# A ReGLU MLP on one core: the first set's x loaded in whole rows and turned on TensorE, later x loaded and turned in quarters of a set

## The chip, the cores and the metric

The kernel runs on one core of a Trainium2 chip. The metric is device time in microseconds (us). Every time quoted without another word is the median of a kernel's runs in one series.

A ratio is the mean time of one kernel's fast runs over the mean of the other's fast runs of the same rounds, so it is not quite the ratio of the medians. It comes with a 95% interval.

PE is TensorE's matmuls, PEld its weight loads, DVE is VectorE, ACT is ScalarE, POOL is GpSimd, and SP is the engine that issues most transfers. A profile is one execution. The profiled run of the kernel before took 369.32 us, longer than each of its timed runs. The span that a profile shows is about 2 us shorter than the device time.

## The reference

```python
batch, seq, dim, hidden = 16, 256, 512, 2048        # x: 16*256 = 4096 tokens, all float32

def reference(x, w1, w2):
    h = x @ w1                                      # 4096x512 @ 512x4096
    gate, value = np.split(h, 2, axis=-1)
    h = np.maximum(gate, 0) * value
    return (h @ w2).astype(np.float32)              # 4096x2048 @ 2048x512
```

## The kernel before

The 4096 tokens are worked in four *sets* of 1024. Each set has two stages.

- **Product blocks.** There are sixteen, one for each 128 hidden columns. A *plain* block does 16 matmuls of 128x512. A *Winograd* block treats (two halves of the tokens) x (gate, value) as a 2x2 product and needs seven products of two matmuls each, 14 in all. For that it needs sums of x (S1 to S4) and of w1 (T1 to T4). The result, after max and multiply, is `g`.
- **The second matmul**, `g` by w2, in tiles named `O`. It is 128 matmuls per set: ten are mixed into the set's own last blocks, 114 form one long run, and four are left to be mixed into the next set's blocks. I call that long run and its surroundings a **set boundary**: from its first matmul to the first product of the next set. During it the next set's x must be brought in, turned and summed.

The matmuls of this kernel take x *turned*: tokens along the row, dimensions on the partitions. Before the change DVE did that with a block transpose, after a load in pieces of 128 numbers (512 bytes).

```python
stage = tile_pool(bufs=1)      # one staging tile: 8 KB per partition, half a set of x
tmp   = tile_pool(bufs=5)      # five temporaries of 4 KB: turned x AND output tiles o
psx = (bufs=3, PSUM); psy = (bufs=3, PSUM); psw = (bufs=2, PSUM)    # X and O share psx

def x_ops(s, eng):                                   # next set's x, at the boundary; eng = POOL
    o = x_tiles()
    t1 = load_x(s, 0, x_tile())                      # first half of the set
    yield o
    a11 = turn(x_tmp(), t1, 0)                       # DVE, 128x1024
    nc.scalar.copy(out=o["A11"], in_=a11)            # ACT
    a12 = turn(x_tmp(), t1, 1)
    nc.scalar.copy(out=o["A12"], in_=a12)
    t2 = load_x(s, 1, x_tile())                      # second half: the SAME staging tile
    yield o
    a21 = turn(x_tmp(), t2, 0)
    a22 = turn(x_tmp(), t2, 1)
    eng.tensor_tensor(o["S1"], a21, a22, op=ADD)     # POOL, reads the turned temporaries
    eng.tensor_tensor(o["S3"], a11, a21, op=SUB)
    nc.scalar.copy(out=o["A22"], in_=a22)            # ACT
    yield o
    eng.tensor_tensor(o["S2"], f(o["S1"]), a11, op=SUB)
    eng.tensor_tensor(o["S4"], a12, f(o["S2"]), op=SUB)
    yield o

# ... mm2_stream: 16 matmuls into one O tile, then
            o = tmp.tile([P, DO], F32, name="o", tag="tmp")
            nc.scalar.copy(out=o, in_=ps)            # ACT
            nc.sync.dma_start(out=out_v[s, b], in_=o)

# ... end of a set
        gen = x_ops(s + 1, nc.gpsimd)
        for xo in gen:
            advance(stream, 10)                      # ten O matmuls, then the next part of x_ops
        advance(stream, NB * NJ - TAIL - 50)
```

The first set starts with four plain blocks, which do not need the sums. (`# ...` marks cuts; the pool lines are shortened.)

## Time and profile before

| | before |
|---|---|
| time | 367.63 us (367.53 to 368.49, 3 runs) |
| TensorE busy | 92% of the span |
| three set boundaries, each needing 24.4 us for its matmuls | 32.38, 31.64, 32.85 us |
| first product of the first set | 13.0 us |
| long O run of the first set begins | 77.1 us |

The first lines are from the profile's page of the kernel before: busy time of the engines, then PE's busy share and granted clock in 40 equal slices, one digit each in tenths.

```profile
PE 339.1 (92%) x1428; PEld 208.9 (57%) x1454; DVE 199.7 (54%) x270; ACT 151.1 (41%) x261; POOL 78.2 (21%) x58
...
PE   7969999996799999999499999999589999999995
PEclk9999999999699999999899999999969999999998
```

After the first set (its start, and stalls at 6 tenths in the third slice), TensorE is nearly always busy except at three spots (6, 4 and 5 tenths), and at or just after each of them its clock falls too. Those spots are the boundaries. The next lines, from the same page, give the chain of work that ended last, and the group of O matmuls: busy us, mean ns of one, then the idle time just before them and what ended it.

```profile
PE 72%; DMA 11%; DVE 7%; POOL 4%; ACT 2%; SPq 2%; issue 1%; DVEq 0%; ACTq 0%
...
L218 PE MATMUL O<-w_sb,g 128*128 128x512 bf16 x500 | 120.5, 396 | 16.6 <-ACT o L230 16.0
```

The waits view of PE gives who waited, for what, total us, number of waits, longest.

```profile
PE O L218 <- ACT o L230: 16.0, 3, 5.4
...
PE X L206 <- ACT x_A_182 L302: 1.3, 1, 1.3
PE X L206 <- ACT x_S_185 L299: 1.1, 1, 1.1
```

"PE waits for ACT's copy of an O tile" is true and misleading: the copy takes 0.58 us and the wait 5.3. One has to look at what stood *in front of* that copy. The timeline of the first boundary shows it (columns: start us, us, engine, line, operation, count; in brackets the idle time of that engine before, and what ended it):

```profile
77.10 11.83 PE L218 MATMUL O<-w_sb,g 128*128 128x512 bf16 x53
...
81.96 1.91 SPq L83 DMA_DIRECT2D xs<-in_x_dram  x4
...
88.67 3.85 DVE L87 STREAM_TRANSPOSE xt<-xs 128x1024 f32<-128x1024 f32 x2 [6.75 <-DMA xs<-in_x_dram]
92.56 1.04 ACT L116 CAST x_A_707<-xt 128x1024 fp32r<-128x1024 f32 x1 [9.55 <-DVE xt L87]
...
93.51 0.58 ACT L230 COPY o<-O 128x512 f32<-128x512 f32 x1
...
94.14 15.70 PE L218 MATMUL O<-w_sb,g 128*128 128x512 bf16 x59 [5.21 <-ACT o L230]
```

Read it from below. PE resumes at 94.14, when the O copy at 93.51 is done. That copy was queued on ACT behind the copy of A22 at 92.56, which ended 9.55 us of idle time. The A22 copy waited for DVE's turn. DVE had idled 6.75 us for the second half of x. That load was issued only at 81.96, because the one staging tile was held by the first half until it was turned. Meanwhile three PSUM tiles of O filled up and PE stopped. In this trace ACT did not let the O copy pass: its tile had long been finished, and it started 0.95 us after the start of the A22 copy and not before it.

### The profile page before, as it was taken

The numbers are of one execution on the slowest core, as the hardware profiler recorded it, in microseconds if no ns is written. First come the engines' busy times: TensorE is split into PE (matmuls) and PEld (weight loads), VectorE is DVE, ScalarE is ACT, GpSimd is POOL, SyncE is SP. The second block draws the span as 40 slices with busy tenths as digits, with TensorE's granted clock in tenths as the row PEclk, the third lists the DMA queues.
The fourth block names the chain that finished last, engine by engine and source line by source line (L and its number), as shares of the span: only waits on it lengthen the run. The fifth ranks groups of instructions, "written<-read, shape, count | busy, mean of one in ns | idle before, by whom it ended". The sixth has DMA issues, their size and how long they took to land.

```text
span 367.5 us, 3904 instructions
## 1 busy us (share of the span) xinstructions
PE 339.1 (92%) x1428; PEld 208.9 (57%) x1454; DVE 199.7 (54%) x270; ACT 151.1 (41%) x261; POOL 78.2 (21%) x58
## 2 busy tenths in 40 slices
PE   7969999996799999999499999999589999999995
PEld 4547566642246777764146777774234777775442
DVE  0588676873005887773402887776400687886000
ACT  2558767520316545522214455542032555552111
POOL 1259989800910000000450000000090000000000
PEclk9999999999699999999899999999969999999998
DMA  9973687905225000006132400001422000000212
GB/s 190 273 221 116 202 206 114 166 29 116 86 86 133 11 0 0 3 0 139 35 114 68 105 2 0 0 2 53 89 87 86 31 0 1 2 0 2 86 62 80
DMA packets 33139, 27.51 MB, mean 75 GB/s; under 512 B 1248, under 2 KB 29152, under 8 KB 33120
## 3 DMA queue, kind: packets, MB, share of 16 engines
q1 hardware_dynamic: 29824, 24.52, 24.6%
q0 software_dynamic: 2112, 2.10, 3.6%
q10 hardware_dynamic: 1184, 0.66, 0.7%
q8 instruction: 11, 0.18, 0.2%
q14 instruction: 8, 0.07, 0.1%
HBM read 20.97 MB, written 8.39 MB: 80 GB/s over the span
## 4 chain that ended last, share of the span: by engine, by line
PE 72%; DMA 11%; DVE 7%; POOL 4%; ACT 2%; SPq 2%; issue 1%; DVEq 0%; ACTq 0%
PE O L218 23%; PE Y L153 22%; PE W L153 14%; PE X L153 13%; DVE xt L87 6%; DMA w_sb<-in_w_dram 6%; DMA xs<-in_x_dram 4%; SPq L83 2%; POOL w_T_84 L135 1%; POOL w_T_85 L136 1%; POOL w_T_87 L138 1%; POOL w_T_86 L137 1%; ACT o L230 0%; ACT w_B_82 L270 0%; ACT x_A_1925 L116 0%
## 5 line engine op out<-in xcount | busy, mean ns | idle before, releaser
L218 PE MATMUL O<-w_sb,g 128*128 128x512 bf16 x500 | 120.5, 396 | 16.6 <-ACT o L230 16.0
L218 PEld LDWEIGHTS <-g 128*128 128x128 bf16 x512 | 50.3, 101 | 83.0 <-issue 31.3
L180 DVE TENSOR_TENSOR cc<-W,pu 128x512 f32<-128x512 f32 x60 | 41.5, 691 | 97.8 <-ACT pu L174 96.0
L160 ACT COPY Y<-X 128x512 f32<-128x512 f32 x60 | 34.3, 572 | 49.7 <-PE X L153 43.3
L174 ACT COPY pu<-Y 128x512 f32<-128x512 f32 x60 | 35.2, 587 | 37.7 <-PE Y L153 37.6
L230 ACT COPY o<-O 128x512 f32<-128x512 f32 x31 | 18.1, 585 | 69.7 <-PE O L218 59.9
L87 DVE STREAM_TRANSPOSE xt<-xs 128x1024 f32<-128x1024 f32 x14 | 27.5, 2000 | 28.5 <-DMA xs<-in_x_dram 28.5
L181 DVE SCALAR_TENSOR_TENSOR g<-X,cc 128x512 bf16<-128x512 f32 x60 | 41.5, 691 | 2.3
L190 DVE SCALAR_TENSOR_TENSOR g<-Y,cc 128x512 bf16<-128x512 f32 x60 | 40.8, 680 | 3.3 <-PE Y L153 3.3
L186 DVE TENSOR_TENSOR cc<-Y,pu 128x512 f32<-128x512 f32 x60 | 40.9, 681 | 0.8 <-PE Y L153 0.3
L167 ACT COPY pu<-W 128x512 f32<-128x512 f32 x60 | 35.2, 587 | 0.0
L114 POOL TENSOR_TENSOR x_S_1317<-xt 128x1024 fp32r<-128x1024 f32 x1 | 2.3, 2341 | 77.8 <-DVE xt L87 77.8
L114 POOL TENSOR_TENSOR x_S_1926<-xt 128x1024 fp32r<-128x1024 f32 x1 | 2.3, 2343 | 76.9 <-DVE xt L87 76.9
L153 PEld LDWEIGHTS <-w_B_82 128*128 128x128 bf16 x120 | 7.2, 98 | 16.6 <-issue 15.9
L227 DVE COPY o<-O 128x256 f32<-128x256 f32 x1 | 0.4, 425 | 25.2 <-ACT o L225 25.2
L153 PE MATMUL Y<-x_S_1318,w_T_85 128*128 128x512 f32 x32 | 13.0, 487 | 0.0
L153 PE MATMUL Y<-x_S_709,w_T_85 128*128 128x512 f32 x32 | 13.0, 487 | 0.0
L153 PE MATMUL Y<-x_S_1927,w_T_85 128*128 128x512 f32 x32 | 13.0, 486 | 0.0
L135 POOL TENSOR_TENSOR w_T_84<-w_sb 128x512 fp32r<-128x512 f32 x6 | 8.7, 1456 | 8.6 <-DMA w_sb<-in_w_dram 8.6
L153 PE MATMUL X<-x_A_1314,w_B_81 128*128 128x512 f32 x32 | 10.3, 404 | 0.0
L153 PE MATMUL X<-x_A_1923,w_B_81 128*128 128x512 f32 x32 | 10.3, 404 | 0.0
L153 PE MATMUL X<-x_A_705,w_B_81 128*128 128x512 f32 x32 | 10.3, 403 | 0.0
(126 smaller groups left out, 509.8 us busy)
## 6 DMA issues: line engine op xcount, KB each, us to landing
out_dram<-o SPq DMA_DIRECT2D x31, 256.0 KB, 2.0
xs<-in_x_dram SPq DMA_DIRECT2D x28, 256.0 KB, 4.9
w_sb<-in_w_dram SPq DMA_DIRECT2D x7, 1024.0 KB, 6.6
w_sb<-in_w_dram POOLq DMA_DIRECT2D x4, 512.0 KB, 9.2
g<-in_x_dram SPq DMA_DIRECT2D x4, 256.0 KB, 8.0
w_sb<-in_w_dram ACTq DMA_DIRECT2D x1, 512.0 KB, 6.5
w_sb<-in_w_dram SPq DMA_DIRECT2D x1, 512.0 KB, 8.6
out_dram<-o ACTq DMA_DIRECT2D x1, 128.0 KB, 1.8
```

Of the source, the lines that this page charges most:

```text
L87: nc.vector.transpose(a.rearrange("p b (tb r) -> p b tb r", r=32), t.rearrange("p tb (c k b) -> p k b tb c", k=2, b=2)[:, k])
L135: nc.gpsimd.tensor_tensor(op["T1"], b12, b11, op=SUB)
L153: nc.tensor.matmul(ps, wop[wn][:, b, self.jb * P:(self.jb + 1) * P], self.xo[xn][:, b, :], start=fresh and b == 0, stop=b == 1, skip_group ...
L160: nc.scalar.copy(out=self.Y, in_=self.X)
L167: nc.scalar.copy(out=self.p5, in_=self.W)
L174: nc.scalar.copy(out=self.u2, in_=self.Y)
L180: nc.vector.tensor_tensor(self.c12, self.W, self.u2, op=ADD)
L181: nc.vector.scalar_tensor_tensor(out=self.g[:, self.jb, :TH], in0=self.X, scalar=0.0, in1=self.c12, op0=MAX, op1=MULT)
L186: nc.vector.tensor_tensor(self.c22, self.Y, self.p5, op=ADD)
L190: nc.vector.scalar_tensor_tensor(out=self.g[:, self.jb, TH:], in0=self.Y, scalar=0.0, in1=self.c22, op0=MAX, op1=MULT)
L218: nc.tensor.matmul(ps, g[:, hc, b * P:(b + 1) * P], w2_sb[:, hc, :], start=hc == 0, stop=hc == NJ - 1)
L230: nc.scalar.copy(out=o, in_=ps)
```

## The change

Its intent: fill the staging earlier and in smaller pieces, so that the boundary has no late load; turn the first set's x on TensorE, which is idle or only warming up then, from loads of whole rows (2 KB); use two plain blocks instead of four. The warm-up matmuls at the start are also changed (30 instead of 38; not shown). The diff, cut to its core:

```diff
-NPLAIN = 4
+NPLAIN = 2
-    stage = ... bufs=1        # 8 KB tile
-    tmp = ... bufs=5
+    stage = ... bufs=3        # 4 KB tiles, a quarter of a set each
+    tmp = ... bufs=4
...
+    HOME = {(0, 0): "A11", (0, 1): "S4", (1, 0): "S3", (1, 1): "A22"}
+    def x_sums(o, engines):          # sums read the copied tiles, not the turned temporaries
+        a11, a22, s1, s2, s3, s4 = (f(o[n]) for n in ("A11", "A22", "S1", "S2", "S3", "S4"))
+        for eng, n, i0, i1, op in zip(engines, ("S1", "S2", "S4", "S3"), (s3, s1, s4, a11), (a22, a11, s2, s3),
+                                      (ADD, SUB, SUB, SUB)):
+            yield eng.tensor_tensor(o[n], i0, i1, op=op)
...
+    def turn_x(o, t, i):             # one quarter: two turns of 128x512, two copies
+        ts = slice(i % 2 * 256, i % 2 * 256 + 256)
+        for k in range(2):
+            a = tmp.tile([P, 2, 256], F32, name="xt", tag="tmp")
+            nc.vector.transpose(a..., t...[:, k])
+            nc.scalar.copy(out=o[HOME[i // 2, k]][:, :, ts], in_=a)
+        if i == 1:
+            nc.scalar.copy(out=o["A12"], in_=f(o["S4"]))
...
+    def turn_first(o, h):            # first set, half h: 16 transposes on TensorE
+        for b in range(4):
+            pool, nm = (psx, "X") if b % 2 else (psw, "W")
+            ps = pool.tile([P, TH], F32, name=nm, tag=nm)
+            for e in range(4):
+                nc.tensor.transpose(ps[:, e * P:(e + 1) * P], xn[h][:, b]...[:, e], ident)
+            for k, copy in ((0, nc.vector.tensor_copy), (1, nc.scalar.copy)):
+                copy(out=o[HOME[h, k]][:, :, b * P:(b + 1) * P], in_=ps[...])
...                                   # preamble: half 0 turned, plain 0 and 1, half 1 turned,
+    sums = x_sums(xo, (nc.vector,) * 4)      # then four sums on DVE among plain 0 and 1
...
+                if n == "P1" and jb in (9, 11, 13) and s + 1 < NS:
+                    xs.append(load_x(s + 1, len(xs)))       # three quarters during the last blocks
...
-            gen = x_ops(s + 1, nc.gpsimd)
-            for xo in gen:
-                advance(stream, 10)
-            advance(stream, NB * NJ - TAIL - 50)
+            xo = x_tiles()
+            turn_x(xo, xs[0], 0)
+            advance(stream, 6)
+            turn_x(xo, xs[1], 1)
+            xs.append(load_x(s + 1, 3))                     # fourth quarter: a staging tile is free now
+            advance(stream, 12)
+            turn_x(xo, xs[2], 2)
+            advance(stream, 18)
+            turn_x(xo, xs[3], 3)
+            for _ in x_sums(xo, (nc.gpsimd,) * 4):
+                pass
+            advance(stream, NB * NJ - TAIL - 46)
```

More of the change, by code (lines that the diff above doesn't have):

```diff
@@ L6 @@
 from concourse._compat import with_exitstack
+from concourse.masks import make_identity
 dt = mybir.dt
@@ L16 @@
 PERIOD = 7
-NWARM = 38
-NPLAIN = 4
+NWARM = 30
+NPLAIN = 2
 SLOT = {"P1": 0, "P5": 1, "P2": 3, "P6": 4, "P3": 5, "P7": 9, "P4": 13}
@@ L44 @@
     gpool = ctx.enter_context(tc.tile_pool(name="gpool", bufs=1))
-    stage = ctx.enter_context(tc.tile_pool(name="stage", bufs=1))
-    tmp = ctx.enter_context(tc.tile_pool(name="tmp", bufs=5))
+    stage = ctx.enter_context(tc.tile_pool(name="stage", bufs=3))
+    tmp = ctx.enter_context(tc.tile_pool(name="tmp", bufs=4))
     psx = ctx.enter_context(tc.tile_pool(name="psx", bufs=3, space=bass.MemoryType.PSUM))
@@ L65 @@
     warm_b = warm.rearrange("p a t -> p (a t)").bitcast(BF16)
-    warm_r = warm.rearrange("p a t -> p (a t)").bitcast(F32R)
-    nc.vector.memset(warm, 0.0)
+    nc.vector.memset(warm[:, 0], 0.0)
+    ident = wpool.tile([P, P], F32, name="ident")
     for i in range(NWARM):
-        pool, nm = (((psy, "Y"),) * 3 + ((psx, "X"),) * 3 + ((psw, "W"),) * 2)[i % 8]
+        pool, nm = (psy, "Y") if i < 16 else (psx, "X")
         t = pool.tile([P, TH], F32, name=nm, tag=nm)
-        m = P // 2 if 18 <= i < 26 else P
-        if i < 10 or i >= 26 and i % 2:
-            nc.tensor.matmul(t, warm_b[:, :P], warm_b[:, :TH], start=True, stop=True)
-        else:
-            nc.tensor.matmul(t[:m], warm_r[:, :m], warm_r[:, TH:], start=True, stop=True)
+        n = TH if i < 16 else TH // 2
+        nc.tensor.matmul(t[:, :n], warm_b[:, :P], warm_b[:, :n], start=True, stop=True)
     def f(ap):
         return ap.bitcast(F32)
-    def load_x(s, h, t):
-        for q in range(4):
-            nc.sync.dma_start(out=t[q * 32:(q + 1) * 32], in_=x_v[s, h, q])
-        return t
-    def turn(a, t, k):
-        nc.vector.transpose(a.rearrange("p b (tb r) -> p b tb r", r=32),
-                            t.rearrange("p tb (c k b) -> p k b tb c", k=2, b=2)[:, k])
-        return a
-    def x_tile():
-        return stage.tile([P, 16, P], F32, name="xs", tag="xs")
-    def x_tmp():
-        return tmp.tile([P, 2, TH], F32, name="xt", tag="tmp")
     def x_tiles():
@@ L99, in x_tiles, with load_x @@
                 for n in ("A11", "A12", "A22", "S1", "S2", "S3", "S4")}
-    def x_ops(s, eng):
-        o = x_tiles()
-        t1 = load_x(s, 0, x_tile())
-        yield o
-        a11 = turn(x_tmp(), t1, 0)
-        nc.scalar.copy(out=o["A11"], in_=a11)
-        a12 = turn(x_tmp(), t1, 1)
-        nc.scalar.copy(out=o["A12"], in_=a12)
-        t2 = load_x(s, 1, x_tile())
-        yield o
-        a21 = turn(x_tmp(), t2, 0)
-        a22 = turn(x_tmp(), t2, 1)
-        eng.tensor_tensor(o["S1"], a21, a22, op=ADD)
-        eng.tensor_tensor(o["S3"], a11, a21, op=SUB)
-        nc.scalar.copy(out=o["A22"], in_=a22)
-        yield o
-        eng.tensor_tensor(o["S2"], f(o["S1"]), a11, op=SUB)
-        eng.tensor_tensor(o["S4"], a12, f(o["S2"]), op=SUB)
-        yield o
+    HOME = {(0, 0): "A11", (0, 1): "S4", (1, 0): "S3", (1, 1): "A22"}
[4 more added lines that the diff above has]
+            yield eng.tensor_tensor(o[n], i0, i1, op=op)
+    def load_x(s, i):
+        t = stage.tile([P, 8, P], F32, name="xs", tag="xs")
+        for q in range(4):
+            nc.sync.dma_start(out=t[q * 32:(q + 1) * 32], in_=x_v[s, i // 2, q, :, i % 2 * 8:i % 2 * 8 + 8])
+        return t
+    def turn_x(o, t, i):
+        ts = slice(i % 2 * 256, i % 2 * 256 + 256)
+        for k in range(2):
+            a = tmp.tile([P, 2, 256], F32, name="xt", tag="tmp")
+            nc.vector.transpose(a.rearrange("p b (tb r) -> p b tb r", r=32),
+                                t.rearrange("p tb (c k b) -> p k b tb c", k=2, b=2)[:, k])
+            nc.scalar.copy(out=o[HOME[i // 2, k]][:, :, ts], in_=a)
+        if i == 1:
+            nc.scalar.copy(out=o["A12"], in_=f(o["S4"]))
     w_stage = w2_sb.rearrange("p hc n -> p (hc n)").bitcast(F32).rearrange("p (u v) -> p u v", u=4)
@@ L274, in plain_w_end, with fetch_first @@
         nc.gpsimd.tensor_tensor(op["T4"], f(op["T4"]), f(op["T2"]), op=SUB)
+    g = g_set[0]
+    x_nat = x2.rearrange("(s h b p) d -> s h b p d", h=2, b=4, p=P)
+    xn = [g[:, 8 + 4 * h:12 + 4 * h].rearrange("p b t -> p (b t)").bitcast(F32).rearrange("p (b d) -> p b d", d=D)
+          for h in range(2)]
+    def fetch_first(h):
+        for b in range(4):
+            nc.sync.dma_start(out=xn[h][:, b], in_=x_nat[0, h, b])
+    def turn_first(o, h):
+        for b in range(4):
+            pool, nm = (psx, "X") if b % 2 else (psw, "W")
+            ps = pool.tile([P, TH], F32, name=nm, tag=nm)
+            for e in range(4):
+                nc.tensor.transpose(ps[:, e * P:(e + 1) * P], xn[h][:, b].rearrange("p (c e) -> p e c", e=4)[:, e], ident)
+            for k, copy in ((0, nc.vector.tensor_copy), (1, nc.scalar.copy)):
+                copy(out=o[HOME[h, k]][:, :, b * P:(b + 1) * P],
+                     in_=ps[:, k * 256:k * 256 + 256].rearrange("p (b t) -> p b t", b=2))
     fetch(0, nc.scalar)
-    t1 = load_x(0, 0, x_tile())
-    late = g_set[0][:, 12:16].rearrange("p b t -> p (b t)").bitcast(F32).rearrange("p (tb c) -> p tb c", c=P)
+    fetch_first(0)
+    make_identity(nc, ident)
     fetch(1, nc.sync)
     fetch(2, nc.sync)
-    t2 = load_x(0, 1, late)
+    fetch_first(1)
     xo = x_tiles()
-    g = g_set[0]
     plain = [Plain(g, jb) for jb in range(NPLAIN)]
@@ L286 @@
     plain_w(0)
-    a11 = turn(x_tmp(), t1, 0)
-    nc.scalar.copy(out=r11, in_=a11)
-    a12 = turn(x_tmp(), t1, 1)
-    nc.scalar.copy(out=r12, in_=a12)
     plain_w(1)
+    turn_first(xo, 0)
+    nc.scalar.copy(out=xo["A12"], in_=f(r12))
     fetch(3, nc.sync)
+    prepare(2)
     plain[0].products(0, r11, r12)
-    a21 = turn(x_tmp(), t2, 0)
-    plain_w(2)
+    copy_some(2)
+    plain[1].products(0, r11, r12)
+    turn_first(xo, 1)
+    copy_some(1)
     fetch(4, nc.sync)
-    plain[1].products(0, r11, r12)
-    a22 = turn(x_tmp(), t2, 1)
-    nc.scalar.copy(out=r21, in_=a21)
-    nc.vector.tensor_tensor(xo["S1"], a21, a22, op=ADD)
-    plain[2].products(0, r11, r12)
-    nc.scalar.copy(out=r22, in_=a22)
     prepare(3)
+    sums = x_sums(xo, (nc.vector,) * 4)
+    next(sums)
+    plain[0].products(1, r21, r22)
+    next(sums)
     copy_some(1)
-    plain[3].products(0, r11, r12)
-    nc.vector.tensor_tensor(xo["S2"], f(xo["S1"]), a11, op=SUB)
-    copy_some(1)
-    plain[0].products(1, r21, r22)
-    copy_some(1)
-    fetch(5, nc.sync)
-    plain[1].products(1, r21, r22)
-    nc.vector.tensor_tensor(xo["S4"], a12, f(xo["S2"]), op=SUB)
-    nc.scalar.copy(out=xo["A12"], in_=a12)
-    prepare(4)
-    copy_some(1)
-    plain[2].products(1, r21, r22)
-    copy_some(1)
-    plain[3].products(1, r21, r22)
-    nc.vector.tensor_tensor(xo["S3"], a11, a21, op=SUB)
-    copy_some(1)
+    plain[1].products(1, r21, r22)
+    next(sums)
+    next(sums)
+    copy_some(2)
     prev = None
@@ L332 @@
         stream = None
+        if s + 1 < NS:
+            xs = []
         last = NJ * PERIOD
-        todo = 4
+        todo = 3
         for at in range(first * PERIOD, (NJ - 1) * PERIOD + 14):
```

## The prediction

> **What bounds the kernel now.** TensorE is busy 92% (page, part 1). The timeline shows a matmul every 0.23 us in the product blocks, every 0.214 us in the second matmul (L218), and three losses.
>
> 1. Set boundaries. From the last block matmul of a set to the first of the next takes 32.4, 31.6 and 32.8 us (77.09-109.46, 164.12-195.73, 250.42-283.25); the 114 L218 matmuls between need 24.4, so 23.6 us are lost. The waits view names O <- ACT o L230, three waits of 5.2 to 5.4 us. Behind it, ACT's queue holds the copy of A22, which waits for a DVE turn, which waits for x, loaded only once the single staging tile was free (81.96; turned from 88.67). Afterwards weight loads stand 0.427 us apart for 3.4 to 5.9 us: half clock, 2 to 3 us more. [...]
> 2. First set: first product at 13.0 us, effectively 14.0; it ends at 77.1. Its 242 matmuls need 55.6 us, so about 8.5 are stalls, mostly at 21 to 34 us.
> 3. The tail, 3.9 us.
>
> **What the change does.**
> - Boundaries: three quarters of x are in SBUF before a set ends; the fourth is loaded once the first is turned. Half-size turns take 1.0 us (2.0 now). I count the last A22 copy at 12 us after the last block matmul, POOL's sums (2.34 each) done at 21, the next block due at 24.4. O copies come late by less than three PSUM tiles cover. No gap, no half clock: 23.1 of 23.6 gained.
> - First set: two plain blocks fewer: 4 matmuls, 0.9 us. Rows of 2 KB should load faster than pieces of 512 B (output rows moved at about 375 GB/s per full DMA share, x at 225). The turn moves to TensorE: 16 transposes per half, each paced by an f32 weight load (0.2 us in the trace), 3.3 us. In the first half they replace DVE turns and copies: products start at 12.5. In the second they add 3.3 us to TensorE. Stalls shrink from 8.5 to 4: x comes sooner, but the first Winograd block waits 2 to 3 us for the four sums, all on DVE (1.2 to 2.1 us each). Set 0 ends at 74.6: gain 2.5 us.
> - The rest: unchanged; four temporary tiles suffice.
>
> **Predicted:** 367.6 - 23.1 - 2.5 = 342.0 us; 8 in 10: 338.5 to 346.5. Faster by over 2%: 0.96; within 2%: 0.03; slower: 0.01.
>
> **What would show it.** Right: waits of O on ACT o near zero; boundary stretches of 24 to 25.5 us; PEclk 9 throughout; 128x512 turns near 1.0 us; first product at 12 to 13 us; transposes 0.15 to 0.25 us apart; first Winograd block waiting on DVE x_S. Wrong: stretches above 26; half clock at 10 to 25 us; waits on w_sb from 23 us on.
>
> **What would make it wrong.** [...] A fourth quarter 3 us late brings back O stalls. Loads of x in blocks 11 and 13 of set 0 share the DMA with w2; O may wait 1 to 2 us once. Transposes much faster than 0.2 us would gain up to 4 us more.

## The result, and the profile after

| | before | after |
|---|---|---|
| time (the three runs above and one more) | 367.58 us (367.31 to 368.49, 4 runs) | 341.12 us (340.65 to 342.32, 4 runs) |
| ratio | | 0.9281 [0.9251, 0.9312] |
| set boundaries | 32.38, 31.64, 32.85 us | 24.43, 24.43, 24.43 us |
| first product | 13.00 us | 11.66 us |
| long O run of the first set begins | 77.10 us | 73.50 us |

The kernel is faster by 26.5 us, and the two profiles differ by 27.3 us of span. Of these, the boundaries give (32.38 + 31.64 + 32.85) - 3 x 24.43 = 23.6 us and the first set 77.10 - 73.50 = 3.6 us. The two make 27.2, so these two places hold the whole difference.

A single profile is not exact at the start. In the kept profiles of the kernels below, the first product came at 10.92 to 12.11 us where the start is that of the change (11.66 here), and at 13.00 to 13.88 where it is that of before. The long O run began at 72.99, 73.08 and 73.50 us in the three profiles with the change's first set (the change, and two kernels of experiments 1 and 4), and at 76.49 to 77.91 in the four with that of before. The two groups stay well apart, but a difference of half a microsecond between the first sets of two profiles means nothing.

The page of the changed kernel, the same lines as before:

```profile
PE 330.7 (97%) x1474; PEld 208.3 (61%) x1474; DVE 199.4 (59%) x290; ACT 157.8 (46%) x285; POOL 77.3 (23%) x58
...
PE   8978999999999999999999999999999999999995
PEclk9999999999999999999999999999999999999999
```

Its chain of work, its O group, and the smaller turns:

```profile
PE 95%; DVE 3%; ACT 0%; issue 0%; ACTq 0%
...
L205 PE MATMUL O<-w_sb,g 128*128 128x512 bf16 x512 | 113.6, 379 | 0.0
...
L103 DVE STREAM_TRANSPOSE xt<-xs 128x512 f32<-128x512 f32 x24 | 24.8, 1112 | 6.3 <-DMA xs<-in_x_dram 6.3
```

The chain is almost TensorE alone (95%), and no O matmul waits (0.0 us instead of 16.6). The waits that are left, in the waits view of PE, lie in the first 30 us:

```profile
PE X L140 <- ACT Y L147: 1.3, 1, 1.3
PE W L140 <- DVE x_S_174 L90: 0.8, 1, 0.8
PE X L193 <- DVE x_S_173 L280: 0.8, 1, 0.8
...
PE Y L140 <- DVE x_S_173 L90: 0.6, 1, 0.6
```

The first boundary of the changed kernel:

```profile
73.50 24.78 PE L205 MATMUL O<-w_sb,g 128*128 128x512 bf16 x114
...
74.30 6.12 DVE L103 STREAM_TRANSPOSE xt<-xs 128x512 f32<-128x512 f32 x6
...
78.10 1.92 SPq L96 DMA_DIRECT2D xs<-in_x_dram  x4
...
84.59 0.62 ACT L105 CAST x_A_752<-xt 128x512 fp32r<-128x512 f32 x1 [0.40 <-DVE xt L103]
...
92.45 2.35 POOL L90 TENSOR_TENSOR x_S_755<-x_A_750,x_S_755 128x1024 fp32r<-128x1024 f32 x1
```

All 114 matmuls run in one piece. DVE turns three quarters at once (six turns from 74.30). The last piece of A22 is copied by 85.2, 11.7 us after the run began. POOL's last sum ends at 92.45 + 2.35 = 94.80, 21.3 us after, while the next set's first product is due at 24.4. So 3.1 us of slack are left.

The start of the changed kernel, PE's part of the timeline:

```profile
9.45 0.64 PE L278 MATMUL X<-ident,g 128*128 128x128 f32 x4
9.93 0.64 PE L278 MATMUL W<-ident,g 128*128 128x128 f32 x4
...
11.66 0.70 PE L193 MATMUL X<-x_A_168,w_B_81 128*128 128x512 f32 x2 [0.61 <-DVE x_A_168 L280]
...
24.39 0.59 PE L140 MATMUL X<-x_A_169,w_B_82 128*128 128x512 bf16 x2 [1.29 <-ACT Y L147]
...
28.51 0.70 PE L140 MATMUL Y<-x_S_173,w_T_86 128*128 128x512 f32 x2 [0.60 <-DVE x_S_173 L90]
```

L278 are the transposes. A group of four comes every 0.48 us, so 0.12 us each, 1.9 us for the sixteen of one half.

### The profile page after: what moved, and what is told of

It reads as the page before. It is cut to its first block, busy times and chain, and to the rows that moved or that the text cites. A ratio compares the mean times of both kernels' runs of the same rounds, so it can differ in the third digit from the quotient of the medians.

```text
span 340.2 us, 4080 instructions
## 1 busy us (share of the span) xinstructions
PE 330.7 (97%) x1474; PEld 208.3 (61%) x1474; DVE 199.4 (59%) x290; ACT 157.8 (46%) x285; POOL 77.3 (23%) x58
## 4 chain that ended last, share of the span: by engine, by line
PE 95%; DVE 3%; ACT 0%; issue 0%; ACTq 0%
PE O L205 33%; PE Y L140 25%; PE W L140 16%; PE X L140 16%; PE Y L73 2%; PE X L193 1%; PE W L193 1%; DVE x_S_173 L90 1%; DVE x_S_172 L90 1%; DVE g L197 1%; DVE x_S_174 L90 0%; PE X L73 0%; DVE x_S_173 L280 0%; ACT v L196 0%; PE W L278 0%; PE X L278 0%
## 5 line engine op out<-in xcount | busy, mean ns | idle before, releaser
L205 PE MATMUL O<-w_sb,g 128*128 128x512 bf16 x512 | 113.6, 379 | 0.0
L167 DVE TENSOR_TENSOR cc<-W,pu 128x512 f32<-128x512 f32 x62 | 42.9, 691 | 85.7 <-ACT pu L161 85.7
L205 PEld LDWEIGHTS <-g 128*128 128x128 bf16 x512 | 48.7, 98 | 61.1 <-issue 4.9
L168 DVE SCALAR_TENSOR_TENSOR g<-X,cc 128x512 bf16<-128x512 f32 x62 | 42.9, 691 | 2.3
L177 DVE SCALAR_TENSOR_TENSOR g<-Y,cc 128x512 bf16<-128x512 f32 x62 | 42.2, 681 | 3.3 <-PE Y L140 3.3
L103 DVE STREAM_TRANSPOSE xt<-xs 128x512 f32<-128x512 f32 x24 | 24.8, 1112 | 6.3 <-DMA xs<-in_x_dram 6.3
L90 POOL TENSOR_TENSOR x_S_1386<-x_S_1388,x_A_1385 128x1024 fp32r<-128x1024 f32 x1 | 2.3, 2347 | 69.8 <-ACT x_A_1385 L105 69.8
L90 POOL TENSOR_TENSOR x_S_2019<-x_S_2021,x_A_2018 128x1024 fp32r<-128x1024 f32 x1 | 2.3, 2347 | 69.3 <-ACT x_A_2018 L105 69.3
L140 PE MATMUL Y<-x_S_1387,w_T_85 128*128 128x512 f32 x32 | 13.0, 487 | 0.0
L140 PE MATMUL Y<-x_S_2020,w_T_85 128*128 128x512 f32 x32 | 13.0, 487 | 0.0
L140 PE MATMUL Y<-x_S_754,w_T_85 128*128 128x512 f32 x32 | 13.0, 486 | 0.0
L140 PE MATMUL Y<-x_S_172,w_T_85 128*128 128x512 f32 x28 | 11.4, 487 | 0.0
L123 POOL TENSOR_TENSOR w_T_85<-w_sb,w_T_84 128x512 fp32r<-128x512 f32 x7 | 10.8, 1539 | 0.6
L140 PE MATMUL X<-x_A_1383,w_B_81 128*128 128x512 f32 x32 | 10.3, 404 | 0.0
```

The source lines that it names most:

```text
L90: yield eng.tensor_tensor(o[n], i0, i1, op=op)
L103: nc.vector.transpose(a.rearrange("p b (tb r) -> p b tb r", r=32), t.rearrange("p tb (c k b) -> p k b tb c", k=2, b=2)[:, k])
L140: nc.tensor.matmul(ps, wop[wn][:, b, self.jb * P:(self.jb + 1) * P], self.xo[xn][:, b, :], start=fresh and b == 0, stop=b == 1, skip_group ...
L167: nc.vector.tensor_tensor(self.c12, self.W, self.u2, op=ADD)
L168: nc.vector.scalar_tensor_tensor(out=self.g[:, self.jb, :TH], in0=self.X, scalar=0.0, in1=self.c12, op0=MAX, op1=MULT)
L177: nc.vector.scalar_tensor_tensor(out=self.g[:, self.jb, TH:], in0=self.Y, scalar=0.0, in1=self.c22, op0=MAX, op1=MULT)
```

## The experiments

Twelve kernels were run, in four series. Each series has its own runs of the kernel before, on the same chip. The median of the kernel before was 367.82 us in the series of experiments 1, 2 and 4, 367.95 in that of 3, 5 and 6, 368.61 in that of the reordered sums (first kernel of 7) and the combined version (8), and 368.15 in that of the two mends and the repair (rest of 7 and 8).

### 1. The boundary part alone, and the first-set part alone

The boundary part alone: the kernel before, with three quarter tiles as staging, the loads during blocks 9, 11 and 13, and the piecewise turn. The first set stays as it was (its first half is staged in the still empty `g`, and three of its turned pieces stay in staging tiles, so that four temporaries suffice).

```diff
-    stage ... bufs=1      -    tmp ... bufs=5
+    stage ... bufs=3      +    tmp ... bufs=4
-            gen = x_ops(s + 1, nc.gpsimd) ...
+            xo = x_tiles(); turn_x(xo, xs[0], 0) ...        # the whole boundary code of the change
```

> Before's first set (its x goes to the late part of g, three of its turned pieces into the staging tiles), the change's set boundaries: x in quarters. Theory: the boundaries alone carry 23.6 us of the gain, so about 344.0 us, boundary stretches of 24.4 us, set 0 still ending at about 77 us. Rival (the new first set is needed for the boundaries to close, or gives a large part of the gain): above 350 us.

Measured: 345.40 us, ratio 0.9384 [0.9356, 0.9411]. The boundaries took 24.43, 24.42 and 24.43 us.

The first-set part alone: the changed kernel with the old boundary code, one 8 KB staging tile and five temporaries.

```diff
-            xo = x_tiles(); turn_x(xo, xs[0], 0) ...
+            gen = x_ops(s + 1, nc.gpsimd) ...               # the old boundary code
```

> The change's first set, before's set boundaries. Theory: set 0 ends at 73.5 instead of 77.1 us and the boundaries stay at 31.6 to 32.8, so about 364.0 us, and the two halves add up to the whole gain. Rival (the parts interact): anything under 361 or over 366.

Measured: 364.29 us, ratio 0.9891 [0.9848, 0.9934]. The boundaries took 32.01, 31.54 and 32.89 us again, with the same 16.0 us of waits for ACT.

The two parts save 6.16% (22.7 us) and 1.09% (4.0 us), together 26.7 us. The whole change saves 7.19% (26.4 us of that length). The parts add up within the intervals, so no sign that one needs or hinders the other, and about six sevenths of the gain is the boundaries.

### 2. How much of a boundary's loss is the gap and how much is the slow clock after it?

In the kernel before, weight loads after a gap stood 0.427 us apart instead of 0.214, for 5.4, 3.4 and 5.9 us at the three boundaries. Half of that time is lost: 7.35 us. The gaps are 16.0 us. That makes 23.4 of the 23.6, on paper. The experiment takes the slow clock away but leaves the gap: in front of the fifth O tile of a set, 24 matmuls nobody uses keep TensorE busy while it would wait.

```diff
+            if b == 4 and not last:
+                fill = psw.tile([P, TH], F32, name="W", tag="W")
+                for _ in range(24):
+                    nc.tensor.matmul(fill, w2_sb[:, 0, :P], w2_sb[:, 1, :], start=True, stop=True)
```

> Before, with 24 matmuls of no use (5.1 us at full clock) put into TensorE's order just before the O matmul that stalls at each of the three boundaries; nothing else is moved. Theory: the gap as such stays, but TensorE stays active, the half clock after it goes, and with it 2.7 + 1.7 + 2.9 = 7.3 us: about 360.3 us. Rival (the slow spacing of 0.427 us after the gap comes from what O waits for, not from the clock): unchanged, 367.5 us.

Measured: 362.59 us, ratio 0.9843 [0.9812, 0.9874], which is 5.8 us. The boundaries took 30.27, 30.38 and 29.85 us, 6.4 us less in sum. The filled gap at the first boundary, on PE's timeline:

```profile
89.57 5.34 PE L220 MATMUL W<-w_sb 128*128 128x512 bf16 x24
95.42 12.89 PE L223 MATMUL O<-w_sb,g 128*128 128x512 bf16 x58 [0.51 <-ACT o L235]
```

The 6 us after the gap, in the windows view (us, then busy time with instructions of PE, PEld, DVE, ACT and POOL, then granted clock, DMA share, GB/s), for the kernel before and for the filled one:

```profile
94.00:100.00 6.00, 5.86 (x16) 2.10 (x16) 0.00 (x0) 1.26 (x3) 5.92 (x4) 0.55 0.35 131
```

```profile
95.00:101.00 6.00, 5.53 (x25) 2.54 (x26) 0.00 (x0) 1.58 (x4) 5.92 (x3) 1.00 0.35 131
```

The granted clock was 0.55 and is 1.00, and 25 matmuls pass where 16 did. So at this boundary half clock followed 5.21 us of idle, and with useless work in the same gap (0.51 us of idle left) it did not come. The rival of no effect (367.5) is out. The size came out 1.5 us short of the 7.3 expected. Part of this is the run and not the clock after the gaps: in that profile the gap ended 0.4 to 0.5 us later at two of the boundaries, and the first set ended 0.8 us later, with 3.4 us at half clock inside it (27.13 to 30.54 us, granted 0.50) that the profile of the kernel before does not have there. So some 6 of the 23.6 us were the clock, by time and by boundaries, 7.3 on paper, and the rest the gap itself.

### 3. Is one copy in ACT's queue the cause of the gap?

The copy of A22 moves from ACT to DVE, so nothing late stands in front of the O copies any more. The staging tile stays single.

```diff
-        nc.scalar.copy(out=o["A22"], in_=a22)
+        nc.vector.tensor_copy(out=o["A22"], in_=a22)
```

> Before with one copy moved: A22 is copied from its turned form by DVE, not ACT, so ACT's queue no longer holds a wait for the late half of x. Theory A (ACT's order is the only thing that holds back the O copies): the gaps go, about 345 us. Theory B (a second thing stands behind it: the O copies also need one of the five temporary tiles, which the turned pieces of x keep until POOL's sums have read them, so the third O copy still waits for the first sum): the gap moves from before the fifth O group to before the sixth and shrinks from 5.3 to about 3.5 us each, about 354 to 360 us. B is my bet, from the O copies of before at 95.05 and 97.35 us, which each follow the end of a POOL sum.

Measured: 362.80 us, ratio 0.9870 [0.9844, 0.9897], only 4.8 us. The first boundary:

```profile
82.26 0.58 ACT L230 COPY o<-O 128x512 f32<-128x512 f32 x1
...
92.28 2.78 POOL L114 TENSOR_TENSOR x_S<-xt 128x1024 fp32r<-128x1024 f32 x1 [19.27 <-DVE xt L87]
95.09 0.59 ACT L230 COPY o<-O 128x512 f32<-128x512 f32 x1 [12.25 <-POOL x_S L114]
95.73 11.34 PE L218 MATMUL O<-w_sb,g 128*128 128x512 bf16 x44 [3.96 <-ACT o L230]
```

The second O copy now runs at 82.26 instead of 93.51, and 70 matmuls pass before the gap instead of 53. Then the third O copy waits 12.25 us, and the line says for whom: POOL's first sum. The output tile `o` and the turned x share the five temporaries. Four of them are held by a11, a12, a21 and a22 until POOL has read them, and POOL cannot start before the late half of x is turned. The gap shrinks from between 5.2 and 5.4 us to between 3.9 and 4.1, and half clock still follows it (granted 0.54 from 180 to 186 us, after the second gap). The direction of theory B is right, that of A (the queue alone) wrong; both expected more than came.

So the gap had two causes one behind the other, **the queue order and the temporaries**, both fed by **the late load**. The change removes all three: the load comes early, and a temporary is free as soon as its copy is made, since the sums read the copies. Which of these would have been enough was not tested: no kernel here only loads the second half earlier and leaves the order of the queue and the temporaries as they were.

### 4. Are three quarters ahead of time needed?

The changed kernel with two staging tiles: two quarters are loaded during the blocks and two at the boundary, each once a tile is free.

```diff
-    stage ... bufs=3
+    stage ... bufs=2
-                if n == "P1" and jb in (9, 11, 13) and s + 1 < NS:
+                if n == "P1" and jb in (9, 11) and s + 1 < NS:
             turn_x(xo, xs[0], 0)
+            xs.append(load_x(s + 1, 2))
```

> The change with two staging tiles of a quarter instead of three: only two quarters are loaded during the last blocks, as many bytes as before held; the third is loaded when the first has been turned, the fourth after the second. Theory (turning in small pieces frees staging early enough; the extra early quarter is not what closes the gap): within 1 us of the change, 341 us, boundaries 24.4 us. Rival (three quarters must be there before the set ends): O waits on ACT for 2 us or more at each boundary, 346 us or more.

Measured: 341.98 us, ratio 0.9288 [0.9262, 0.9315]. The boundaries took 24.58, 24.43 and 24.42 us. That is the same as the change within the interval, with 4 KB per partition less. So a third quarter ahead of time is not needed, and two quarters, the 8 KB that the staging of before held, are enough. Whether it is the smaller pieces or the temporaries freed early that makes them enough, this run does not separate.

Its profile has one more thing to teach. In the first set, with no wait over 1.3 us, TensorE was busy 1.72 of 3.40 us, and half clock followed (windows view, columns as in experiment 2):

```profile
22.00:25.40 3.40, 1.72 (x6) 0.86 (x6) 3.40 (x4) 3.29 (x7) 3.40 (x2) 1.00 0.45 157
25.44:28.85 3.41, 3.41 (x9) 2.07 (x8) 3.25 (x4) 1.62 (x4) 3.33 (x3) 0.50 0.36 94
```

So here half clock followed several short waits close together. In the change's profile it did not: there a stretch with 1.71 of 3.41 us busy (from 23.53) kept 1.00. Half clock of 3.4 us in the first set, starting between 25.0 and 27.1 us, also stands in the profiles of experiments 1 (boundary part), 2 and 3.

### 5. What do transposes on TensorE cost, and do they lower the clock?

Each of the 32 transposes of the first set is made four times, so 96 are added, and 64 stand in a row.

```diff
-            for e in range(4):
+            for e in [0, 1, 2, 3] * 4:
```

> The change with every TensorE transpose issued four times (the same result): 96 more. Theory (each costs its spacing of 0.12 us on TensorE's own time, and they keep the clock up): 96 x 0.12 = 11.5 us more at most, less what the first set's waits for weights and sums get back, so 349 to 353 us, with a granted clock of 1.0 throughout. Rival ([...] 64 of them in a row, 7.7 us, halve the clock): matmuls 0.43 us apart after the transposes, granted clock under 1.0 between 10 and 30 us, 355 us or more.

Measured: 351.16 us, ratio 0.9552 [0.9534, 0.9569], 10.0 us more than the change by medians of two series. The two stretches of 64 transposes, in the windows view with columns as above:

```profile
9.00:17.00 8.00, 7.84 (x65) 7.65 (x64) 1.39 (x4) 1.83 (x5) 5.34 (x6) 1.00 1.08 360
21.00:29.00 8.00, 8.00 (x66) 7.89 (x64) 1.97 (x4) 1.91 (x5) 2.10 (x2) 1.00 0.00 0
```

The clock stays 1.00 in both, so two stretches of 64 transposes did not lower it. The 64 transposes take 7.7 us, so one every 0.12 us, as in the change. The lines view gives the duration of one (the second number after the bar, in ns):

```profile
L278 PE MATMUL W<-ident,g 128*128 128x128 f32 x64 | 8.4, 284 | 0.0
```

So a transpose lasts 284 ns from start to end (the profile models the ends of matmuls), but the next one starts 0.12 us after it: they overlap, and what a row of them costs is the distance of their starts. The 96 added ones would cost 11.5 us; about 1.5 us came back: the first Winograd block no longer waited for the sums.

### 6. Do two plain blocks serve better than four?

The changed kernel with four plain blocks: four matmuls more (0.9 us), but the sums are not needed so soon.

```diff
-NPLAIN = 2
+NPLAIN = 4
     # preamble: four plain products per half, the four sums spread among the second four
-        todo = 3
+        todo = 4
```

> The change with four plain blocks again instead of two (weights of blocks 2 and 3 plain at first, their sums at the end of the set). Theory (the two plain blocks fewer are worth their 4 matmuls less, 0.9 us, but bring the first Winograd block forward onto the four sums of x, about 2.9 us of waits): four plain blocks hide the sums and cost 0.9 us, about 339 us. Rival (as the change intends, two are better): 342 us or more.

Measured: 340.80 us, ratio 0.9269 [0.9248, 0.9289]. Neither expectation came true: it is the same as the change. The waits for the sums are gone from PE's waits (the longest wait left on a DVE sum or a Y copy is 0.3 us), which makes up for the four matmuls. In the profiles the long O run of the first set even began sooner, at 72.09 us, but the times do not tell the two kernels apart. No gain from this part of the change can be seen.

### 7. Can the waits of the first Winograd block be removed?

In the changed kernel, DVE's sums take 1.78, 2.28, 1.69 and 2.30 us beside POOL's sums of w1. Alone (in the transposes' experiment) they take 1.22. My estimate from these times was that the sums would fall to about 1.2 us without POOL beside them. I therefore put S1 and S2 on DVE with nothing on POOL, S4 on DVE, S3 on POOL, and POOL's sums of the next piece of w1 after that.

```diff
-    prepare(3)                                  # POOL's four sums of w1, then DVE's four sums of x
-    sums = x_sums(xo, (nc.vector,) * 4)
+    copies.extend(w1_copies(jb3, n3, t3)); copy_some(3)
+    nc.vector.tensor_tensor(xo["S1"], ...); nc.vector.tensor_tensor(xo["S2"], ...)
     plain[0].products(1, r21, r22)
+    nc.vector.tensor_tensor(xo["S4"], ...)
     plain[1].products(1, r21, r22)
+    nc.gpsimd.tensor_tensor(xo["S3"], ...)
+    w1_sums(jb3, n3, t3)                        # POOL's sums of w1, now last
```

> The change with the first set's four sums of x rearranged: the first two back to back on DVE, the fourth on POOL ahead of the sums of the weights of blocks 4 and 5 (which so start after it and run less beside DVE), and ACT's weight copies ahead of the plain block's eviction. Theory (the first Winograd block waits for these sums and for an ACT copy, 2.9 us in all, and DVE's sums take 1.7 to 2.3 us because POOL works beside them): about 2 to 2.5 us faster than the change, 338.6 to 339.2 us, DVE sums near 1.2 us. Rival (the weights then come late and give it back): 340.5 us or more, with waits on POOL's weight sums or on w2 later in the set.

Measured: 345.78 us, ratio 0.9384 [0.9358, 0.9409]: slower than the change by about 1% of the time before, against my theory. The timeline, later than where I had looked:

```profile
29.36 5.61 SPq L114 DMA_DIRECT2D w_sb<-in_w_dram  x2
...
34.95 1.14 ACT L128 CAST w_B<-w_sb 128x512 fp32r<-128x512 f32 x2 [5.03 <-DMA w_sb<-in_w_dram]
...
36.00 0.58 ACT L163 COPY pu<-Y 128x512 f32<-128x512 f32 x1
...
36.72 1.19 PE L142 MATMUL Y<-x_S,w_T 128*128 128x512 f32 x2 [4.11 <-ACT pu L163]
```

What I aimed at worked in part: S1 and S2 took 1.23 us each, and two products of the first block came 1.8 and 2.6 us sooner (0.5 us of that was there from the first product on, at 11.12 instead of 11.66 us, before anything that the edit moves). But POOL's delayed sums held the staging of w1 longer, so the next load of w1 was issued only at 29.36. The copies of that load stood in ACT's queue in front of the copy of Y that PE needed, and PE waited 4.1 us; the next pairs of matmuls then ran at half clock (granted 0.50 from 37 to 40 us), the float32 pairs 0.85 us apart instead of 0.46. It is the mechanism of the boundaries again, made by my own edit. S4 met POOL's S3 and took 3.01 us: S3 ran from 20.84 to 23.23, and S4, begun at 21.3, ended at 24.31, 1.08 us after it. What in POOL's work slows DVE no run here shows.

Two mends of it followed. The first issues the copies of w1 at other places in the blocks, later in the row:

```diff
-                if n in ("P2", "P7"):
+                if n in (("P6", "P3") if jb % 2 else ("P4",)):
                     copy_some(1)
```

> e_sums with one more edit: ACT's copies of the weights of blocks 6 to 15 stand eight product slots (about 3.7 us) later in ACT's order. e_sums gained 2.6 us in the first Winograd block (its P7 at 25.9 instead of 28.5 us) and lost 4.5 us at 32 us, where an ACT copy waited for weights from memory and the copies of the products behind it waited too. Theory (the loss is ACT's order, as at the set boundaries): the wait at 32 us falls below 1 us, about 339 us, unless w2, whose load follows POOL's weight sums, now comes late for O and costs up to 2 us. Rival (POOL's weight sums themselves are too late): a wait of TensorE on POOL's sums in their place, 343 us or more.

Measured: 342.18 us, ratio 0.9292 [0.9264, 0.9319]. The long wait is gone, but a new one stands in PE's waits:

```profile
PE X L142 <- ACT Y L149: 2.4, 6, 0.5
```

Six times, three weight copies in a row (1.66 us on ACT) stand in front of a copy into Y. These 2.4 us are about what had been gained, so I take the gain to be spent there; it was not tested further.

The second leaves the change's queues alone and only moves DVE's sums ahead of the plain blocks' evictions:

```diff
+    copy_some(3)
     next(sums)
-    plain[0].products(1, r21, r22)
     next(sums)
-    copy_some(1)
-    plain[1].products(1, r21, r22)
+    plain[0].products(1, r21, r22)
     next(sums)
+    plain[1].matmuls(1, r21, r22)
     next(sums)
-    copy_some(2)
+    plain[1].evict(1)
```

> The change with the four sums of x left on DVE and POOL's weight sums left where they are; only DVE's order (first two sums back to back, the fourth ahead of plain block 1's eviction) and ACT's weight copies of blocks 4 and 5 (ahead of the evictions) are moved. The sums still run beside POOL at 1.7 to 2.3 us. Theory: about 1 us of the 2.9 us gained, 340 us, no new wait for weights. Rival (order doesn't matter, only the contended length of the sums): the same as the change, 341 us.

Measured: 341.42 us, ratio 0.9273 [0.9249, 0.9296], the same as the change. The wait for Y fell to 0.3 us, but the two waits on sums stayed (0.9 and 0.6 us) since POOL still worked beside them.

### 8. A combined version, with a wrong result

This one, on top of experiment 7, uses ten fewer warm-up matmuls, transposes in the Y tiles of PSUM so that X and W are free, and evicts later.

```diff
-NWARM = 30
+NWARM = 20
-            pool, nm = (psx, "X") if b % 2 else (psw, "W")
-            ps = pool.tile([P, TH], F32, name=nm, tag=nm)
+            ps = psy.tile([P, TH], F32, name="Y", tag="Y")
```

> e_sums, and a shorter start: ten warm-up matmuls fewer (in the change the transposes start only when the warm-up ends, 8.9 us), the weight copies of block 1 behind the copies of the transposes on ACT, the transposes into the idle Y tiles, and those of the second half copied ahead of the eviction of plain block 1. Theory: first product at 10.6 instead of 11.66 us, 0.8 us of wait gone before the second half, so 1.5 to 2 us faster than e_sums, about 337 us. Rival (the start is bound by the arrival of x and of weights): first product above 11.3 us, no faster than e_sums.

Measured: 345.37 us, ratio 0.9367 [0.9341, 0.9393], and the result was **wrong** (relative error 0.2195), which I had not expected. The first product came at 11.13 us, no sooner than in experiment 7 with its thirty warm-ups (11.12; 12.11 in its first mend): the transposes began only 0.1 us sooner (8.23 instead of 8.34 us), and around 9.9 us they came more slowly for about 0.2 us, where the fourth group needs the Y tile of the first, which ACT was still copying. What bounds the start between 8 and 11 us is left open.

For the wrong result I had a guess that can be checked. A Winograd block lets ACT write Y and then lets TensorE *add* to it. In this kernel the last matmul into a Y bank before that is a transpose, which covers only 128 of the bank's 512 columns. The guess: in the other 384 columns the block's first product, which ACT wrote, is overwritten where it should be added to. In the change the last matmuls into Y before the blocks are the sixteen full-width warm-up matmuls, and its result is right. (These sixteen are still there in this kernel, since the ten dropped ones wrote to X; the transposes came after them.) To test it I put three full-width matmuls into Y after the transposes:

```diff
     turn_first(xo, 1)
+    for _ in range(3):
+        t = psy.tile([P, TH], F32, name="Y", tag="Y")
+        nc.tensor.matmul(t, warm_b[:, :P], warm_b[:, :TH], start=True, stop=True)
```

> e_best, which gave a wrong result, with three full-width matmuls of zeros, each starting a new sum, put onto the three Y banks after the transposes. Theory (the Winograd blocks let TensorE add onto a Y tile that ACT wrote; [...]): the result is correct again. Rival (another fault of e_best): still wrong. Its time, near 345 us as e_best, is of no interest.

Measured, one look: still wrong, relative error 0.1283 (345.65 us, state unknown). In the built program the three matmuls had gone to only two of the three Y banks, one of them twice. So the guess can be put to the numbers. By it, 384 columns of the first Y of each bank (the first three Winograd blocks of the first set) lose their first product in the first kernel, and in the repaired one only those of the third of these blocks. The reference's formula, computed afterwards on a host with the reference's inputs and with the block's first product left out of Y in just these columns, is wrong by 0.2195 and by 0.1283: the two measured errors to four digits (the first or the second block alone would give 0.1261 or 0.1250). That leaves little room for another fault, but what in the bank makes the add an overwrite was not shown. A run with all three banks covered and a right result was not made.

No version beat the change: two staging tiles, four plain blocks, the moved sums and the first mend of experiment 7 are the same within the intervals.

## Why the prediction was right or wrong

The time (342.0 predicted, 341.12 measured) was right, and so was its main term. Point by point:

- **Boundaries: right.** Predicted 23.1 of 23.6 us gained; in the profiles 23.6, by the boundary part alone 22.7. No O matmul waits, the clock is full throughout the profiled run (0.995 to 1.000 in the four), and every stretch is 24.43 us. The counts inside held too: last A22 copy at 12 us (11.7), POOL's sums done at 21 (21.3), turns near 1.0 us (1.02 and 1.07 in the first boundary, 1.11 in the mean of all).
- **Half clock: right, at the lower end.** "2 to 3 us more" per boundary stood in the prediction; with the gap filled, the boundaries were 6.4 us shorter, or 2.1 each, and the time 5.8 us.
- **The chain behind the wait: right, but not complete.** The prediction named the queue order and the late load. It did not name the temporaries held until POOL's sums, which the experiment with the A22 copy on DVE showed as a second barrier right behind. The change removed both, so this cost the prediction nothing.
- **First set: the direction right, the size too small.** Predicted gain 2.5 us; measured 3.6 in the profile and 4.0 by the first-set part alone. The largest mis-sized term is the transposes: "each paced by an f32 weight load (0.2 us in the trace), 3.3 us" per half. They came 0.12 us apart, 1.9 us per half. The weight load's own duration (0.21 us here) is not the distance between two of them. The prediction had named this as a risk ("much faster than 0.2 us"). Part of the surplus cancelled: by the prediction's own sum (238 matmuls need 54.7 us, the second half's transposes 1.9), the stalls between the first product and the O run were 5.2 us where it had 4. So the start came 0.8 us sooner, the transposes cost 1.4 less, the stalls 1.2 more; that the total came so near 342.0 owes a little to luck.
- **First product:** predicted 12.5 us, measured 11.66, for the same reason as far as the profile tells (10.92 to 12.11 in the kernels with the same start), and then no stall inside the first plain block, where the kernel before had one of 0.68 us.
- **Waits of the first Winograd block: the amount right, the reason half right.** "2 to 3 us for the four sums": 1.3 + 0.8 + 0.6 = 2.7 us. But the largest, 1.3, was for ACT's copy of Y, which waited its turn in ACT's queue (with the weight copies issued ahead of it, in the last mend of experiment 7, it fell to 0.3); only 1.4 was for sums.
- **Two plain blocks fewer: 0.9 us counted, nothing net.** With four plain blocks the time was 340.80, the same within the intervals: the four matmuls saved are spent again as waits for the sums.
- **Risks that did not come:** the fourth quarter was not late (last A22 copy at 11.7 us), and O did not wait (0.0 us) while x shared the DMA with w2. Nor did the transposes lower the clock (1.00 in two rows of 64, experiment 5).
- **Faster loads:** the eight loads of the first set's x took 5.8 us to land (median), those of the second half took 8.0 before, and all transfers together (x and weights) moved 248 and 356 GB/s in the first and second 8 us instead of 187 and 280. No experiment changed the row length alone, so how much of the first set's gain this is stays open.

## What to carry to other kernels

When a matmul "waits for a copy" that is far shorter than the wait, read what stood in front of the copy in its engine's queue and which buffer it needed: here one copy on ACT, waiting 9.55 us for a late load, held up the copy of a finished O tile behind it, and with it PE for 5.21 us, and removing that barrier uncovered the next (temporaries held until POOL's sum, 3.9 to 4.1 us of PE; in my own edit a held staging tile, 4.1 us). Loading earlier and freeing buffers in small pieces, with later readers pointed at the copies, cured this here at little cost; two quarter tiles did as well as three. A gap on TensorE costs more than its length when half clock follows it, as here (3.4 to 5.9 us of it after gaps of 5.2 to 5.4 us). What the row of transposes cost was the distance of their starts, not the duration of one (0.12 and 0.28 us), so measure the distance. And where matmuls add to a PSUM tile that ACT wrote, the result here was right after full-width warm-up matmuls in the banks and wrong (relative errors 0.2195 and 0.1283) after transposes in them, so check results when anything new is put into such a bank.
